# The order list of the attention and convolution stage, written anew

## The chip, the cores and the metric

The kernel runs on one core of one Trainium2 chip. The metric is the device time of one execution in microseconds (us). The profile shows five engines: TensorE (PE, with its weight loads as PEld), VectorE (DVE), ScalarE (ACT), GpSimd (POOL) and SyncE (SP), which here issues the transfers. Each engine works through its own instructions in order; semaphores connect them. Times inside the execution are counted from the start of the profiled span.

## The reference

One layer of a diffusion backbone is computed in float32 for 128 context tokens and 512 latent tokens of width 1024. In its middle stands a mixer that runs attention and a short convolution side by side on the same projection:

```python
q = _rms(q.reshape(b, s, N_HEADS, HEAD_DIM), q_norm)     # 8 heads of 64, 2 kv heads
k = _rms(k.reshape(b, s, N_KV, HEAD_DIM), k_norm)
...
attn = _block_attention(q_r, k_all, v_all)               # blocks of 128 queries, 640 keys for latents
y_conv = gb * _short_conv(gc * u, conv_w)                # width 3, 512 channels
merged = jnp.concatenate([_rms(attn, attn_out_norm), _rms(y_conv, conv_out_norm)], axis=-1)
return merged @ w_out, k, v
```

Around it, `_layer` computes the modulation `mod = silu(cond) @ w_ada + b_ada` (called ada below), two normalisations, and a SwiGLU feed-forward part with the weights `w_gate_up` and `w_down`. The context reads only context keys; latent queries attend to 128 cached context keys and 512 latent keys in one softmax.

## The kernel before

Every float32 product of large matrices is made of three matmuls of values split into a rounded high part and a remainder (`wh`/`wl` for weights, `hH`/`hL` for tokens; `split`, L150 to L152, writes the high part on ACT and the rest on DVE). The program has four stages: loading, ada and the query projection; then attention and convolution mixed; then the output projection; then the feed-forward part, which takes more than half of the time. The change lies in the second stage alone, which runs from about 60 to 256 us.

In that stage the order of TensorE's work is written out by hand in the string `SEQ` (L39 to L49). A loop at the end of the stage's code walks through it and calls one function for each entry:

```python
for x in SEQ.split():
    if "." in x:
        n, i = (int(y) for y in x[1:].split("."))
        {"S": att_s, "T": att_t, "O": att_o}[x[0]](units[n], i)
    else:
        steps[x[0]](int(x[1:]))
```

TensorE follows the list to the letter. What the steps ask of ACT, DVE, POOL and SP is put in order by a scheduler that goes by priorities, so a step moved in the list may also move work on those engines among other work. The entries are:

- `k0` to `k4`: keys and values of one block of 128 tokens (4 is the context): 24 matmuls (`kv_mm`), the norm of the heads, the split `osq` (L659 on ACT, L660 on DVE), and the store of the values. `c0` does the split alone for the cached keys (`ck`). `K` and `C` turn the split keys by transposes (L667) into `KA`/`KB`, evicted at L669 and L670.
- `q` splits the queries (no TensorE work), `Q` turns them (L703, evicted by ACT at L704).
- `a`, `t`, `o`: attention of the context (scores L917, exponential L928, transposes L936, products L947).
- `Su.h`: scores of unit u (16 units: four blocks, two kv heads, two pairs of heads each) for the head h of its pair (L835). DVE takes the max (L841), ACT scales it (L842) and takes the exponential (L845), DVE the reciprocal (L847), and the scaling is done on DVE for head 0 (L851), on ACT for head 1 (L849).
- `Tu.g`: transposes of the probabilities (L862) for key blocks 0 and 1, 2 and 3, or 4, and their split `ph`/`pl`.
- `Ou.g`: products with the values (L879). Behind `Ou.2` ACT evicts the unit (L886). Each second unit ends its pair of units: two transfers `es` on SP (L894, L895) exchange the halves of the partitions, DVE adds (L900, L901), ACT squares (L902).
- `r`: the row sums of the squares (L954) with the chain of the inverse root behind it, which starts with `ms` (L163).
- `F1`: the next filler from the convolution (L723 to L725; nine, nine and six matmuls for each half of the tokens) or a piece of ada (L394, L446, L785). Their order among themselves is fixed.

Few PSUM buffers are to be had: one score tile `ps` (so the next `S` waits until the exponential has read the one before), two tiles `pt` for all transposes, one `po`, three `pc`. Of `ph` and `pl` there are two each.

Of the kernel before, what the change touches and what calls it, by code (L numbers as in the profile page):

```python
# [37 lines left out]
XB = 3  # L38
SEQ = ('k1 c0 q4 k4 C0 k0 K4 Q4 q0 a0 F1 k2 a1 K0 t0 k3 t1 o0 K1 F1 Q0 o1 K2 F1 K3 F1 S0.0 F1 F1 S0.1 '  # L39
# [10 lines left out]
GCUT = [0, 6, 12, 17, 22]  # L50
GB = 3
SOP = [20, 0]
# [39 lines left out]
def build(ctx, tc, x_prompt, x_sample, c, cache_k, cache_v, c_ctx, norm_mix, norm_ffn, w_ada, b_ada,  # L92
# [875 lines left out]
    def rms_of(t):  # L968
        if t == CTX or t >= 0:
# [5 lines left out]
             "a": ctx_s, "t": ctx_t, "o": ctx_o, "r": att_rms}  # L975
    for x in SEQ.split():
        if "." in x:
# [404 lines left out]
```

## Time and profile before

| what | us |
| --- | --- |
| median of 3 runs | 751.99 (751.41 to 752.06) |
| the profiled execution | 752.85 |
| its span, first to last instruction | 751.1 |
| PE busy | 732.7 |
| PEld busy | 657.4 |
| DVE busy | 529.0 |
| ACT busy | 374.8 |
| POOL busy | 49.2 |

The granted clock of TensorE was 1.000. Busy times are sums over the whole span. In the rows of a timeline the columns are the start, the duration, the engine, the line, the operation with the tiles written and read, and in brackets the idle time before it and what ended that. A row of waits names who waited, for whom, the total, the number of times and the longest.

### The profile page before, as it was taken

The page shows a single profiled execution, that of the slowest core. Times are in us where ns is not written, and L with a number is a line of the kernel's source. Part 1 is how long each engine was busy: PE and PEld are TensorE (multiplying, and loading weights), DVE is VectorE, ACT ScalarE, POOL GpSimd, SP SyncE. Part 2 cuts the span into 40 slices and gives each one's busy share as a digit, 9 for nine tenths or more (in the row PEclk, how much of TensorE's full clock was granted, in tenths as well). Part 3 has the DMA queues.
Part 4 walks back from the last instruction along what each step waited for, and adds up shares of the span by engine and source line. Part 5 has one row for each costly group of instructions (what it writes and reads, how often), then busy time and mean ns, then how long its engine had stood idle before and what let it go on. Part 6 is the DMA issues. An engine that isn't in the chain of part 4 may idle for free.

```text
span 751.1 us, 11645 instructions
## 1 busy us (share of the span) xinstructions
PE 732.7 (98%) x4556; PEld 657.4 (88%) x4556; DVE 529.0 (70%) x905; ACT 374.8 (50%) x701; POOL 49.2 (7%) x85
## 2 busy tenths in 40 slices
PE   7899989999999999999999999999999999999997
PEld 5568878988988887899998799998889998899986
DVE  5557877676666798788868768765568766677653
ACT  5346878667666534775552135553125641255510
POOL 2402201011010120100000000000000000000000
PEclk9999999999999999999999999999999999999999
DMA  9995133522532464032325313233113132123312
GB/s 288 275 251 174 43 113 93 175 92 93 165 102 92 134 230 135 1 113 56 111 65 197 91 57 113 57 113 120 49 57 109 61 113 84 57 65 104 100 69 85
DMA packets 101387, 84.50 MB, mean 113 GB/s; under 512 B 3502, under 2 KB 81650, under 8 KB 101332
## 3 DMA queue, kind: packets, MB, share of 16 engines
q1 hardware_dynamic: 100980, 83.39, 36.1%
q0 software_dynamic: 352, 0.37, 0.4%
q8 instruction: 36, 0.59, 0.3%
q14 instruction: 19, 0.16, 0.1%
HBM read 79.68 MB, written 2.75 MB: 110 GB/s over the span
## 4 chain that ended last, share of the span: by engine, by line
PE 85%; DVE 4%; ACT 4%; DMA 4%; issue 1%; SPq 1%; POOL 0%; ACTq 0%
PE pf L155 19%; PE pf L156 19%; PE pf L157 19%; PE pc L723 3%; PE pc L725 3%; PE pc L724 3%; PE po L879 2%; PE pt L862 2%; PE ps L835 2%; PE pc L394 2%; PE ph L156 2%; PE ph L157 2%; PE ph L155 2%; DMA af<-in_w_ada_dram 1%; SPq L329 1%
## 5 line engine op out<-in xcount | busy, mean ns | idle before, releaser
L151 ACT ACTIVATE wh<-wf 128x1024 fp32r<-128x1024 f32 (+1 forms) x68 | 65.8, 970 | 109.4 <-PE pf L157 69.3
L152 DVE TENSOR_TENSOR wl<-wf,wh 128x1024 fp32r<-128x1024 f32 (+1 forms) x58 | 68.6, 1185 | 59.9 <-ACT wh L151 46.2
L155 PE MATMUL pf<-B,wh 128*128 128x320 f32 x288 | 89.1, 310 | 0.0
L157 PE MATMUL pf<-B,wl 128*128 128x320 f32 x288 | 89.1, 309 | 0.0
L156 PE MATMUL pf<-B,wh 128*128 128x320 f32 x288 | 89.0, 309 | 0.0
L155 PE MATMUL pf<-wh,gT 128*128 128x512 f32 (+1 forms) x225 | 86.9, 386 | 0.0
L155 PE MATMUL pf<-T,wh 128*128 128x320 f32 x280 | 86.8, 310 | 0.0
L156 PE MATMUL pf<-wl,gT 128*128 128x512 f32 (+1 forms) x225 | 86.5, 385 | 0.0
L156 PE MATMUL pf<-T,wh 128*128 128x320 f32 x280 | 86.5, 309 | 0.0
L157 PE MATMUL pf<-T,wl 128*128 128x320 f32 x280 | 86.5, 309 | 0.0
L157 PE MATMUL pf<-wh,gT 128*128 128x512 f32 (+1 forms) x225 | 86.5, 384 | 0.0
L151 ACT ACTIVATE wh<-sx 128x1024 fp32r<-128x1024 f32 x40 | 42.4, 1060 | 61.6 <-DVE sx L206 22.8
L152 DVE TENSOR_TENSOR wl<-sx,wh 128x1024 fp32r<-128x1024 f32 x40 | 49.0, 1224 | 28.2 <-ACT wh L151 24.7
L723 PE MATMUL pc<-hH,wh 128*128 128x320 f32 x192 | 61.1, 318 | 0.0
L725 PE MATMUL pc<-hH,wl 128*128 128x320 f32 x192 | 59.3, 309 | 0.0
L724 PE MATMUL pc<-hL,wh 128*128 128x320 f32 x192 | 59.3, 309 | 0.0
L157 PEld LDWEIGHTS pf<-B,wl 128*128 128x128 f32 x288 | 54.1, 188 | 0.1
L155 PEld LDWEIGHTS pf<-B,wh 128*128 128x128 f32 x288 | 54.1, 188 | 0.1
L156 PEld LDWEIGHTS pf<-B,wh 128*128 128x128 f32 x288 | 54.1, 188 | 0.1
L155 PEld LDWEIGHTS pf<-T,wh 128*128 128x128 f32 x280 | 52.5, 188 | 0.7 <-ACT u L1212 0.4
L156 PEld LDWEIGHTS pf<-T,wh 128*128 128x128 f32 x280 | 52.6, 188 | 0.0
L157 PEld LDWEIGHTS pf<-T,wl 128*128 128x128 f32 x280 | 52.6, 188 | 0.0
(302 smaller groups left out, 1670.0 us busy)
## 6 DMA issues: line engine op xcount, KB each, us to landing
wf<-in_w_gate_up_dram SPq DMA_DIRECT2D x44, 512.0 KB, 4.1
aw<-in_w_ada_dram SPq DMA_DIRECT2D x24, 512.0 KB, 4.0
wf<-in_w_down_dram SPq DMA_DIRECT2D x20, 512.0 KB, 3.8
wf<-in_w_in_dram SPq DMA_DIRECT2D x18, 512.0 KB, 5.5
af<-in_w_ada_dram SPq DMA_DIRECT2D x32, 256.0 KB, 6.3
x<-in_x_sample_dram SPq DMA_DIRECT2D x8, 512.0 KB, 6.1
wf<-in_w_out_dram SPq DMA_DIRECT2D x8, 512.0 KB, 4.3
wf<-in_w_ada_dram SPq DMA_DIRECT2D x8, 512.0 KB, 3.7
```

The source lines that it names most:

```text
L151: act.activation(hi, src, AF.Copy)
L152: dve.tensor_tensor(lo, src, f32(hi), ALU.subtract)
L155: pe.matmul(out, lh, rh, start=start, stop=False, skip_group_check=more)
L156: pe.matmul(out, lh, rl, start=False, stop=False, skip_group_check=more)
L157: pe.matmul(out, ll, rh, start=False, stop=stop, skip_group_check=more)
L394: pe.matmul(out[CG * g:CG * (g + 1)], cp[:, k], w, start=(k < 4), stop=(k >= KD - 4), skip_group_check=True)
L723: pe.matmul(acc, wh[:, k], hH[k][:, c0:c0 + n], start=(k == 0), stop=False)
L724: pe.matmul(acc, wh[:, k], hL[k][:, c0:c0 + n], start=False, stop=False)
L725: pe.matmul(acc, wl[:, k], hH[k][:, c0:c0 + n], start=False, stop=(k == KD - 1))
L835: pe.matmul(s2[:, g, :320], q, kk[:, v, P + g * 320:P + (g + 1) * 320], start=(i == 0), stop=(i == 1))
L862: pe.transpose(tp[:, i, h], u[3][h][:, kt * P:(kt + 1) * P], ident)
L879: pe.matmul(ov, w, x[:, i].rearrange("p a q -> p (a q)"), start=(g == 0 and i == 0 and n == 0), stop=(last and i == len(kts) - 1 and n == 1))
```

## The change

The string `SEQ` is replaced. It has the same 244 entries, 84 of them `F1`; some fifty stand one to four places earlier or later. No function, size or buffer is changed. Its beginning and one line of its end:

```diff
-SEQ = ('k1 c0 q4 k4 C0 k0 K4 Q4 q0 a0 F1 k2 a1 K0 t0 k3 t1 o0 K1 F1 Q0 o1 K2 F1 K3 F1 S0.0 F1 F1 S0.1 '
-       'q1 F1 F1 S1.0 F1 T0.0 S1.1 T0.1 T0.2 O0.0 F1 O0.1 O0.2 S2.0 T1.0 F1 T1.1 T1.2 S2.1 O1.0 F1 F1 '
...
-       'O12.2 S14.0 T13.0 T13.1 F1 S14.1 F1 F1 T13.2 F1 O13.0 F1 O13.1 S15.0 F1 F1 O13.2 S15.1 r2 T14.0 '
...
+SEQ = ('c0 k1 q4 k4 C0 k0 K4 Q4 a0 q0 F1 k2 K0 a1 t0 k3 t1 K1 o0 F1 Q0 o1 K2 K3 q1 F1 S0.0 F1 F1 F1 S0.1 F1 '
+       'F1 S1.0 T0.0 F1 S1.1 T0.1 T0.2 O0.0 F1 O0.1 O0.2 S2.0 T1.0 F1 T1.1 T1.2 S2.1 O1.0 F1 F1 r4 S3.0 Q1 '
...
+       'S13.0 O11.2 T12.0 T12.1 F1 O12.0 F1 S13.1 F1 T12.2 O12.1 F1 S14.0 T13.0 T13.1 F1 O12.2 F1 S14.1 F1 '
+       'O13.0 F1 O13.1 T13.2 S15.0 F1 r2 F1 T14.0 S15.1 O13.2 T14.1 F1 F1 F1 T14.2 F1 F1 F1 O14.0 O14.1 '
...
```

Three places show what becomes of it on the engines.

The first is the head of the latent attention. On TensorE, from K2 to S0.0 (`osq_1015` is the split of block 2, `osq_1097` of block 3; `ps_1201` and `ps_1208` are the score tiles of S0.0), the rows were

```order
L667 MATMUL pt_1170<-identr_210,osq_1015 128x128 x4
L723 MATMUL pc_963<-hH_57_199,wh_686 128x320
L724 MATMUL pc_963<-hL_65_207,wh_686 128x320
L725 MATMUL pc_963<-hH_57_199,wl_687 128x320
L723 MATMUL pc_963<-hH_58_200,wh_686 128x320
L724 MATMUL pc_963<-hL_66_208,wh_686 128x320
L725 MATMUL pc_963<-hH_58_200,wl_687 128x320
L667 MATMUL pt_1184<-identr_210,osq_1097 128x128 x4
```

and are now, again on TensorE from K2 on,

```order
L667 MATMUL pt_1170<-identr_210,osq_1015 128x128 x4
L667 MATMUL pt_1177<-identr_210,osq_1097 128x128 x4
L723 MATMUL pc_963<-hH_57_199,wh_686 128x320
L724 MATMUL pc_963<-hL_65_207,wh_686 128x320
L725 MATMUL pc_963<-hH_57_199,wl_687 128x320
L723 MATMUL pc_963<-hH_58_200,wh_686 128x320
L724 MATMUL pc_963<-hL_66_208,wh_686 128x320
L725 MATMUL pc_963<-hH_58_200,wl_687 128x320
L835 MATMUL ps_1208<-KA_729,qT_1142 128x320 x2
```

The six matmuls of the filler moved from between the two turns to behind them, and S0.0 follows at once.

On DVE at the same place, around the max of S0.0 (L841; `wl_1478` and `wl_1484` are the low parts of the same weights), the rows were

```order
L152 TENSOR_TENSOR m_176_737<-of_1119,m_175_736 128x256
L152 TENSOR_TENSOR wl_1478<-wf_1475,wh_1477 128x1024
L841 TENSOR_REDUCE nsr_1206<-ps_1201 128x1
L900 TENSOR_TENSOR of_1119<-t_267_1158,es_1160 64x256
L901 TENSOR_TENSOR of_1119<-t_267_1158,es_1160 64x256
L847 RECIPROCAL nsr_1206<-nsr_1206 128x1
L851 TENSOR_SCALAR pr_1209<-pr_1209,nsr_1206 128x640
```

and on DVE they are now

```order
L152 TENSOR_TENSOR m_176_737<-of_1126,m_175_736 128x256
L841 TENSOR_REDUCE nsr_1213<-ps_1208 128x1
L643 TENSOR_TENSOR pl_1194<-of_698,tab_589 128x16x16
L900 TENSOR_TENSOR of_1126<-t_267_1158,es_1160 64x256
L901 TENSOR_TENSOR of_1126<-t_267_1158,es_1160 64x256
L645 TENSOR_TENSOR pr_1192<-pr_1192,pl_1194 128x512
L847 RECIPROCAL nsr_1213<-nsr_1213 128x1
L152 TENSOR_TENSOR wl_1484<-wf_1481,wh_1483 128x1024
L851 TENSOR_SCALAR pr_1216<-pr_1216,nsr_1213 128x640
```

The weights' low part moved from ahead of the max to between the reciprocal and the scaling; two steps of the rotary positions (L643, L645) of `q1` came in between.

The second place is the end of unit 11. On SP, this piece of the difference shows the two transfers `es` of units 10 and 11 and the loads around them:

```order
-L228 DMA aw_2745<-in_w_ada_dram 128x2x512
-L228 DMA aw_2749<-in_w_ada_dram 128x2x512
-L894 DMA es_2768<-t_584_2631 64x2x128
-L895 DMA es_2768<-t_584_2631 64x2x128
+L228 DMA aw_2734<-in_w_ada_dram 128x2x512
+L228 DMA aw_2738<-in_w_ada_dram 128x2x512
 L228 DMA wf_3113<-in_w_out_dram 128x2x512
-L228 DMA aw_2927<-in_w_ada_dram 128x2x512
-L228 DMA aw_2931<-in_w_ada_dram 128x2x512
+L894 DMA es_2779<-t_593_2668 64x2x128
+L895 DMA es_2779<-t_593_2668 64x2x128
```

The load `wf_3113` of the output weights stood behind the two transfers and stands ahead of them now.

On DVE the rows from the max of S13.0 to that of S13.1 (`ps_2753` and `ps_2826` are their scores; L252 makes the low part of output weights) were

```order
L841 TENSOR_REDUCE nsr_2758<-ps_2753 128x1
L252 SCALAR_TENSOR_TENSOR wl_3090<-wf_3087,vec_187,wh_3089 128x512 x2
L847 RECIPROCAL nsr_2758<-nsr_2758 128x1
L851 TENSOR_SCALAR pr_2761<-pr_2761,nsr_2758 128x640
L152 TENSOR_TENSOR pl_2793<-pt_2787,ph_2792 128x512
L152 TENSOR_TENSOR pl_2802<-pt_2796,ph_2801 128x512
L900 TENSOR_TENSOR of_2523<-t_584_2631,es_2768 64x256
L152 TENSOR_TENSOR pl_2823<-pt_2819,ph_2822 128x256
L841 TENSOR_REDUCE nsr_2831<-ps_2826 128x1
```

and on DVE they are now, from the two L252 to the same max,

```order
L252 SCALAR_TENSOR_TENSOR wl_3090<-wf_3087,vec_187,wh_3089 128x512 x2
L841 TENSOR_REDUCE nsr_2769<-ps_2764 128x1
L152 TENSOR_TENSOR pl_2793<-pt_2787,ph_2792 128x512
L152 TENSOR_TENSOR pl_2802<-pt_2796,ph_2801 128x512
L847 RECIPROCAL nsr_2769<-nsr_2769 128x1
L851 TENSOR_SCALAR pr_2772<-pr_2772,nsr_2769 128x640
L900 TENSOR_TENSOR of_2523<-t_593_2668,es_2779 64x256
L841 TENSOR_REDUCE nsr_2831<-ps_2826 128x1
```

The two L252 moved ahead of S13.0's max, and the split `pl_2823` of T12.2, which stood between the addition (L900) and S13.1's max, is gone from there.

The third place is r2 (L954) on TensorE. Its rows from the products of O13.2 to the second tile of T14 (`pt_3044`) were

```order
L835 MATMUL ps_3017<-KA_729,qT_2492 128x320 x2
L835 MATMUL ps_3017<-KB_730,qT_2492 128x320 x2
L954 MATMUL pt_3029<-ones_174,osq_2524 128x1
L862 MATMUL pt_3035<-ident_77,pr_2871 128x128
L862 MATMUL pt_3035<-ident_77,pr_2910 128x128
L862 MATMUL pt_3035<-ident_77,pr_2871 128x128
L862 MATMUL pt_3035<-ident_77,pr_2910 128x128
L862 MATMUL pt_3044<-ident_77,pr_2871 128x128
```

and on TensorE they are now, from r2 to the first transpose of T14.0,

```order
L954 MATMUL pt_2996<-ones_174,osq_2524 128x1
L723 MATMUL pc_3002<-hH_51_193,wh_2730 128x320
L724 MATMUL pc_3002<-hL_59_201,wh_2730 128x320
L725 MATMUL pc_3002<-hH_51_193,wl_2731 128x320
L723 MATMUL pc_3002<-hH_52_194,wh_2730 128x320
L724 MATMUL pc_3002<-hL_60_202,wh_2730 128x320
L725 MATMUL pc_3002<-hH_52_194,wl_2731 128x320
L723 MATMUL pc_3002<-hH_53_195,wh_2730 128x320
L724 MATMUL pc_3002<-hL_61_203,wh_2730 128x320
L725 MATMUL pc_3002<-hH_53_195,wl_2731 128x320
L862 MATMUL pt_3012<-ident_77,pr_2876 128x128
```

A filler of nine matmuls now stands between r2 and T14.0, whose two tiles came right behind r2 before.

15 rows, old and new, of the table SEQ are left out of this document.

## The prediction

> **What bounds the kernel now.** I read the page first (its first rows and its chain), then a table of windows over the stage that the list orders, then TensorE's waits there.
>
> ```profile
> span 751.1 us, 11645 instructions
> PE 732.7 (98%) x4556; PEld 657.4 (88%) x4556; DVE 529.0 (70%) x905; ACT 374.8 (50%) x701; POOL 49.2 (7%) x85
> PE 85%; DVE 4%; ACT 4%; DMA 4%; issue 1%; SPq 1%; POOL 0%; ACTq 0%
> ```
>
> TensorE is busy for all but 18.4 us, and 85% of the chain that ended last is its own. A new order of the same work can only win from those 18.4 us, and only from the part that lies in this stage. The windows below give span, then busy time (and count) of PE, PEld, DVE, ACT and POOL, the granted clock, the DMA share and GB/s. The stage runs from about 60 to 256 us.
>
> ```profile
> 60.00:92.00 32.00, 29.23 (x229) 27.31 (x227) 25.80 (x81) 24.18 (x65) 9.43 (x12) 1.00 0.30 87
> 92.00:111.00 19.00, 16.86 (x113) 14.24 (x113) 15.46 (x28) 13.09 (x28) 1.52 (x2) 1.00 0.39 118
> 111.00:200.00 89.00, 88.88 (x641) 79.55 (x640) 59.76 (x121) 63.91 (x137) 10.54 (x19) 1.00 0.36 114
> 200.00:256.00 56.00, 54.95 (x393) 48.63 (x393) 37.30 (x77) 35.50 (x77) 3.58 (x9) 1.00 0.38 123
> 256.00:291.00 35.00, 34.40 (x158) 27.85 (x156) 33.63 (x56) 18.02 (x35) 7.21 (x6) 1.00 0.58 194
> ```
>
> PE's idle time is 2.77 + 2.14 + 0.12 + 1.05 = 6.1 us in the stage, most of it before 111 us. Behind the stage DVE is 96% busy for 35 us. What PE waits for in the stage (total, times, longest):
>
> ```profile
> PE ps L835 <- ACT pr L845: 2.4, 4, 1.0
> PE pt L703 <- ACT qT L704: 1.0, 1, 1.0
> PE pt L936 <- ACT wh L151: 0.7, 1, 0.7
> PE pt L862 <- DVE ms L163: 0.4, 1, 0.4
> PE ps L917 <- ACT pr L928: 0.3, 1, 0.3
> PE pt L667 <- ACT osq L659: 0.3, 1, 0.3
> PE pt L667 <- DVE osq L660: 0.2, 1, 0.2
> ```
>
> The largest is the score step S (L835) that waits for the exponential of the score before (L845), since there is one score tile. Matmul ends are modelled, so short stalls show only as gaps of the weight loads. These rows of PEld are for 92 to 111, 111 to 160, 160 to 200, and the last two for 200 to 256 us:
>
> ```profile
> PEld ps L835 <- ACT pr L845: 2.9, 4, 1.2
> ...
> PEld ps L835 <- ACT pr L845: 0.5, 2, 0.4
> ...
> PEld ps L835 <- ACT pr L845: 0.2, 1, 0.2
> ...
> PEld ps L835 <- ACT pr L845: 0.9, 2, 0.7
> ...
> PEld pt L862 <- DVE ms L163: 0.6, 1, 0.6
> ```
>
> **The change, part by part.** Nothing is added or removed: 244 entries each, and the same 84 fillers. A filler is 9 or 6 matmuls of the convolution, or a piece of ada. What is moved changes what I call cover: PE's work between a step and the step that needs its result. The price of a place is latency minus cover.
>
> *The head, to T0.0.* The rows that carry it:
>
> ```profile
> 66.44 0.40 ACT L659 ACTIVATE osq<-ck 128x256 fp32r<-128x256 f32 x1
> 69.97 0.43 DVE L660 TENSOR_TENSOR osq<-pr,osq 128x256 fp32r<-128x256 f32 x1 [0.28 <-ACT osq L659]
> 89.23 0.43 DVE L660 TENSOR_TENSOR osq<-pr,osq 128x256 fp32r<-128x256 f32 x1
> 89.78 0.46 PE L667 MATMUL pt<-identr,osq 128*128 128x128 f32 x4
> 92.15 1.22 DVE L152 TENSOR_TENSOR wl<-wf,wh 128x1024 fp32r<-128x1024 f32 x1
> 93.28 0.82 DVE L841 TENSOR_REDUCE nsr<-ps 128x1 f32<-128x640 f32 x1
> 94.11 0.31 PE L724 MATMUL pc<-hL,wh 128*128 128x320 f32 x1
> 94.25 0.31 PE L725 MATMUL pc<-hH,wl 128*128 128x320 f32 x1
> 94.52 0.88 ACT L845 ACTIVATE pr<-ps,nsr,rq 128x640 f32<-128x640 f32 x1
> 95.55 0.56 PE L835 MATMUL ps<-KA,qT 128*128 128x320 f32 x2 [0.99 <-ACT pr L845]
> 95.95 0.45 PE L835 MATMUL ps<-KB,qT 128*128 128x320 f32 x2
> 99.73 0.83 ACT L849 ACTIVATE pr<-pr,nsr 128x640 f32<-128x640 f32 x1 [0.50 <-DVE nsr L847]
> ```
>
> Step c0 (the cached keys' split) comes first, so `osq<-ck` moves ahead of the stage on ACT and DVE; C0 no longer waits (0.3 + 0.2 us). K4, behind k0, then arrives that much earlier and its own osq (done at 70.40) is soon the limit: I take 0.5 us of the gain through to Q4 and bound it by 0.2 and 0.8. K0 goes ahead of a1 and fills its 0.3 us wait, but that takes 0.3 us of cover from t1, whose wait of 0.7 us stays: 0 to 0.3, I take 0.3. So t1 starts 0.8 us earlier.
>
> K3 now stands right behind K2 with no filler between. K3's osq ended at 89.66 while its matmuls began at 89.78, and the six matmuls taken out are 6 x 0.147 = 0.9 us (0.147 is the distance of matmul starts where they run behind one another: nine take 1.3). Of the 0.9 the slack of 0.1 goes off: 0.8 if the osq moves with PE. Its ACT half stands behind the evictions of Q0, so it will move less: I take a stall of 1.0, bounds 0.3 and 1.2. That gives back the gain: +0.2.
>
> Then S0.0. Before, its max (L841) stood behind a 1.22 us split (L152 `wl`) on DVE; the split is now behind the reciprocal, so the max starts up to 0.9 us sooner, and three fillers stand between S0.0 and S0.1 instead of two (cover 2.2 to 3.5 us). S0.1 began at 95.55 after 0.99 us of idling: this stall goes, and with the weight load's share (the longest of PEld's four) it is 1.2, which brings the head to −1.0. The split now delays S0.0's normalisation by 1.2 us, which nobody needs before T0.0. T0.0 itself moves ahead of a filler, right behind S1.0; the L849 that it needs ended at 100.56, 4.2 us behind S0.1's matmuls (95.95 + 0.45), and its cover falls from 4.7 to 3.3: a new stall of 0.8 to 1.0. It fills the time in which S1.1 used to wait for S1.0's exponential (of PEld's 2.9 us I give it 0.9). Of PEld's 2.9 us in four waits, 2.9 − 1.2 − 0.9 = 0.8 is left, at S1.0 and S2.0; with the earlier max it shrinks by some 0.6. Head: −0.5 −0.3 +1.0 −1.2 +0.0 −0.6 = **−1.6** (bounds −2.8 and 0).
>
> *Middle and r2.* Between S6.0 and S6.1 one filler more (2.3 to 3.6 us of cover): the 0.4 us wait goes. S10.0 moves behind two fillers and T9's transposes (2.4 to 5.8): 0.2 goes. r2, the row sums before T14.0, moves one filler (1.3 us) ahead, so the 0.6 us wait of T14.1's tile for `ms` (L163) goes; I take 0.5. Covers that shrink stay over the exponential's latency, which was 2.1 us from the max's start (93.28) to L845's end (95.40) at S0.0 and up to 0.9 more where the max waits, 2.1 to 3.0: S7.1 to S8.0 falls from 5.7 to 3.5, S11.1 to S12.0 from 5.1 to 3.1, S14.1 to S15.0 from 6.0 to 3.7. Cost nothing there; if that cover is gone, see the first rival. Term: −0.4 −0.2 −0.5 = **−1.1** (−1.5 and −0.3).
>
> *S12 to S14.* SP now issues a 512 KB load ahead of the two `es` transfers of units 10 and 11, ACT both halves of L251 ahead of the eviction (L886) that they need, and DVE L900 directly ahead of S13.1's max.
>
> ```profile
> DMA to landing us min/median/max: 2.0/2.4/4.5
> 215.19 0.88 SPq L228 DMA_DIRECT2D aw<-in_w_ada_dram  x2
> 216.70 0.60 SPq L894 DMA_DIRECT2D es<-t  x1
> 218.15 0.44 SPq L228 DMA_DIRECT2D wf<-in_w_out_dram  x1
> 216.57 0.71 ACT L251 ACTIVATE wh<-wf,vec 128x512 fp32r<-128x512 f32 x1
> 221.22 0.42 DVE L900 TENSOR_TENSOR of<-t,es 64x256 f32<-64x256 f32 x1 [0.76 <-DMA es<-t]
> 221.90 0.81 DVE L841 TENSOR_REDUCE nsr<-ps 128x1 f32<-128x640 f32 x1
> 228.10 0.56 PE L835 MATMUL ps<-KA,qT 128*128 128x320 f32 x2 [0.46 <-ACT pr L845]
> ```
>
> Behind two loads this `es` took 4.5 us (216.70 to 221.2) against a median of 2.4, so about 1.05 per load. Now 0.7 (L251) + 0.4 (the load's issue) + 1.05 (a third load) = 2.2 us later, or 1.1 if queues do not add. L900's end moves from 221.64 to 222.7 or 223.8, and L841 with it, less the 0.4 us split that stood between them. S14.0 needs S13.1's exponential; its cover grows by 0.3. So S14.0 stalls 0.4 to 1.5 us, I take 0.8. Against it S14.1's wait goes (0.7 by its weight load), having one filler more, and T13.0 keeps its wait. Term: +0.8 −0.7, about **0** (−1.1 and +1.2). In the Trainium skill, "DMA: Bandwidth & Descriptors", section "Queues, rings and completion order", descriptors of one issuing engine are consumed in ring order on each DMA engine; by that the full 2.2 us counts and the sum would be 0.7 us worse. The trace agrees as far as the 4.5 us landing behind two loads goes.
>
> *Behind the stage* order and work stay nearly the same: 0. DVE's near-full stretch (33.63 of 35.00 us) starts with work that waits for the last O and the last convolution, so it starts earlier with the stage's end; 0.6 us of PE idling there bounds it, −0.3 to +0.6.
>
> Sum: −1.6 −1.1 +0 +0 = −2.7. The profiled execution took 752.85 us (span 751.1 and 1.75 around it), 0.86 above the median of 751.99; 752.85 − 2.7 = 750.15 there, and 749.3 as a median.
>
> **The rivals.** *Covers too short* (slower). The list shortens some ten distances, T7.0's from 6.3 to 4.1, T0.0's from 4.7 to 3.3, the score steps above, and at O8.0, O9.0 and O12.0 the time for the eviction between two units from 2.4 to 3.9 down to 2.0 to 2.2. T0.0's needed latency of 4.2 shows that such distances can bind. If ACT and DVE serve them 0.5 us later than now at nine places, 4.5 us come back: −2.7 + 4.5 = +1.8, **753.8**. It decides (no gain) from 0.3 us a place. For it: ACT and DVE are 76% and 81% busy from 60 to 92 us. Against it: from 111 to 200 us they are 72% and 67% busy, and PE idles 0.12 us in 89.
>
> *The gain is absorbed* (same). DVE at 96% from 256 to 291 us could be the bound whenever the stage ends; then all that is won before turns into waiting there, **752.0**. For it: the DVE row. Against it: PE is 98% busy in the same 35 us, so DVE is not ahead of it by being the only limit.
>
> *Only the head works.* The S12 to S14 term comes out at its bad end, +1.2, and r2's wait moves on to the next reader of that tile (+0.5): −2.7 + 1.2 + 0.5 = −1.0, **751.0**, hardly measurable.
>
> **How the numbers follow.** A measurement of this kernel can tell about 0.2%, 1.5 us. Forecast (749.3, its own range 747.4 to 750.5) 0.58; covers too short 0.22; absorbed 0.10; only the head 0.10. The head at its good end and the rest as summed give 752.0 − 1.2 − 2.7 = 748.1, with the middle and S12 to S14 good too 746.6; I put the low end at 747.2. The high end takes in about half of the first rival, up to +1.5: 753.5. Faster: 0.58 and a fifth of the last case, 0.60; slower: the first rival and a little of the others, 0.24; same 0.16.
>
> **What would show it.** Right: no wait at C0 or S0.1, a wait of about 1 us at K3 (L667) and at T0.0 (L862 for L849), L835's total for L845 down from 2.4 to about 1.5, none at L862 for L163; `es` of units 10 and 11 landing 1 to 2 us later and S14.0 waiting. Wrong: waits of L835, L862 or L879 between 111 and 200 us, where there were none; a stage shorter by over 2 us while the span stays (absorbed); PE waits for `wl` (L252) behind 256 us.

## The result, and the profile after

The changed kernel took 747.49 us (median of 4 runs, 747.37 to 747.79) against 751.99 us (751.41 to 752.06): the ratio is 0.9942, with a 95% interval of 0.9925 to 0.996. It is 4.5 us faster. The forecast was 2.7 us faster, 749.3; the time lies in the stated range (747.2 to 753.5), near its low end. One later run of the kernel before took 2537.83 us and stands in no ratio below.

The page of the profiled execution after, the same rows as before:

```profile
span 745.8 us, 11640 instructions
PE 729.5 (98%) x4556; PEld 657.5 (88%) x4556; DVE 529.8 (71%) x905; ACT 375.6 (50%) x701; POOL 48.6 (7%) x85
PE 85%; DVE 6%; DMA 3%; ACT 3%; issue 2%; POOL 1%; SPq 0%; ACTq 0%; DVEq 0%; POOLq 0%
```

Work and bound are the same; only PE's idle time is less. The windows after, with the columns as in the prediction:

```profile
60.00:92.00 32.00, 29.26 (x227) 27.27 (x226) 26.89 (x83) 23.58 (x64) 9.45 (x12) 1.00 0.28 76
92.00:111.00 19.00, 17.34 (x121) 15.17 (x120) 14.51 (x26) 13.74 (x31) 2.07 (x2) 1.00 0.35 111
111.00:200.00 89.00, 89.00 (x647) 79.87 (x646) 62.13 (x125) 65.16 (x138) 10.05 (x19) 1.00 0.38 117
200.00:256.00 56.00, 55.05 (x389) 49.91 (x388) 38.23 (x76) 38.07 (x81) 5.92 (x11) 1.00 0.41 132
```

Idle time in the second and fourth windows fell little (2.14 to 1.66 us, 1.05 to 0.95), in the first hardly at all. The windows are fixed in time while the work in them moved, so they do not show the gain well. What shows it is where the stage begins and ends. Its first matmul, and the first one behind its last step, stand here, first of before, then of after:

```profile
60.69 0.28 PE L155 MATMUL pc<-wh,hH 128*128 128x256 f32 x1
255.66 0.39 PE L155 MATMUL ph<-wh,m 128*128 128x512 f32 x1
```

```profile
59.26 0.28 PE L155 MATMUL pc<-wh,hH 128*128 128x256 f32 x1
251.01 0.39 PE L155 MATMUL ph<-wh,m 128*128 128x512 f32 x1
```

Before, the stage took 255.66 − 60.69 = 194.97 us; after, 251.01 − 59.26 = 191.75. That is 3.2 of the 5.3 us by which the two spans differ, and 0.6 more lie behind the stage. The other 1.4 us lie ahead of it, where neither list has a say, and the profiles name 1.1 of them: waits for the ada pieces of the loading stage. First before, then after, for 20 to 60 us:

```profile
PE pc L394 <- DMA af<-in_w_ada_dram: 1.9, 3, 1.2
```

```profile
PE pc L394 <- DMA af<-in_w_ada_dram: 0.8, 1, 0.8
```

That is one execution against another: in the twelve runs below the stage begins at 59.2 to 59.8 us, with the old beginning of the list as with the new. The profiled execution of before was a late one, 0.86 us over its median. So I compare stages by their length, and whole kernels by medians.

What PE waits for in the stage after (total, times, longest):

```profile
PE pt L936 <- ACT wh L151: 0.9, 1, 0.9
PE pc L723 <- DVE modt L448: 0.9, 1, 0.9
PE ps L835 <- ACT pr L845: 0.9, 1, 0.9
PE pt L862 <- ACT pr L849: 0.7, 1, 0.7
PE pt L703 <- ACT qT L704: 0.7, 1, 0.7
PE ps L835 <- DVE KB L670: 0.3, 1, 0.3
PE pt L667 <- ACT osq L659: 0.3, 1, 0.3
PE pt L703 <- DVE pl L152: 0.2, 1, 0.2
```

The score step's waits for the exponential fell from four (2.4 us) to one (0.9). T14.1's wait for `ms` (L163) and C0's are gone; the 0.3 us for `osq` are K3's now (forecast). Three more are new: L862 for L849 (T0.0, forecast), L835 for `KB` (S0.0, not forecast), and L723 for `modt` (a filler behind T14.2, not forecast).

### The profile page after: what moved, and what is told of

Read it like the earlier page. It is cut to its first block, busy times and chain, and to the rows that moved or that the text cites. A ratio compares the mean times of both kernels' runs of the same rounds, so it can differ in the third digit from the quotient of the medians.

```text
span 745.8 us, 11640 instructions
## 1 busy us (share of the span) xinstructions
PE 729.5 (98%) x4556; PEld 657.5 (88%) x4556; DVE 529.8 (71%) x905; ACT 375.6 (50%) x701; POOL 48.6 (7%) x85
## 4 chain that ended last, share of the span: by engine, by line
PE 85%; DVE 6%; DMA 3%; ACT 3%; issue 2%; POOL 1%; SPq 0%; ACTq 0%; DVEq 0%; POOLq 0%
PE pf L155 19%; PE pf L156 19%; PE pf L157 19%; PE pc L723 3%; PE pc L725 3%; PE pc L724 3%; PE pt L862 3%; PE po L879 2%; PE ps L835 2%; PE pc L394 2%; PE ph L156 1%; PE ph L157 1%; PE ph L155 1%; DMA es<-t 1%; DMA af<-in_w_ada_dram 1%
## 5 line engine op out<-in xcount | busy, mean ns | idle before, releaser
L152 DVE TENSOR_TENSOR wl<-wf,wh 128x1024 fp32r<-128x1024 f32 (+1 forms) x58 | 69.2, 1195 | 59.2 <-ACT wh L151 45.2
L723 PE MATMUL pc<-hH,wh 128*128 128x320 f32 x192 | 61.0, 318 | 0.9 <-DVE modt L448 0.9
L156 PEld LDWEIGHTS pf<-T,wh 128*128 128x128 f32 x280 | 52.6, 188 | 0.0
```

The costliest lines, as they stand in the source:

```text
L152: dve.tensor_tensor(lo, src, f32(hi), ALU.subtract)
L156: pe.matmul(out, lh, rl, start=False, stop=False, skip_group_check=more)
L723: pe.matmul(acc, wh[:, k], hH[k][:, c0:c0 + n], start=(k == 0), stop=False)
```

## Experiments

The parts of the new list were put into the kernel before, one at a time, cut where both lists have handled the same steps. Behind S14.1 the count of fillers has to come out even: before, two stand there, in p_late and p_cov none, in p_end three, and in the changed kernel one. Beside the medians (each against the kernel before on the same chip; the ratios are worked out from all runs, not from the medians) stands the length of the stage in the profiled execution, 194.97 before and 191.75 after.

| kernel | what it has | median, us | against before, us | ratio (95%) | stage, us |
| --- | --- | --- | --- | --- | --- |
| p_swap | entries 1 and 2 new | 751.36 | −0.57 | 0.9991 (0.9982 to 1.0000) | 194.65 |
| p_head | entries 3 to 52 new | 752.23 | +0.30 | 1.0003 (0.9994 to 1.0012) | 195.10 |
| p_headswap | entries 1 to 52 new | 751.04 | −0.96 | 0.9991 (0.9981 to 1.0000) | 194.82 |
| p_mid | to O8.1 new | 751.13 | −0.80 | 0.9989 (0.9979 to 0.9998) | 194.38 |
| p_late | S10.0 to S14.1 new | 750.07 | −1.86 | 0.9976 (0.9966 to 0.9986) | 193.18 |
| p_es | S10.0 to O11.2 new | 751.03 | −0.97 | 0.9988 (0.9978 to 0.9997) | 194.26 |
| p_cov | T12.0 to S14.1 new | 750.73 | −1.27 | 0.9982 (0.9973 to 0.9992) | 193.78 |
| p_end | behind S14.1 new | 751.36 | −0.92 | 0.9992 (0.9983 to 1.0001) | 194.96 |
| after_again | all new | 747.93 | −4.49 | 0.9940 (0.9926 to 0.9953) | 191.66 |
| a_o13 | all new, O13.2 earlier | 747.15 | −4.85 | 0.9940 (0.9922 to 0.9959) | 190.93 |
| a_k3b | all new, a filler back at K3 | 747.18 | −5.10 | 0.9936 (0.9920 to 0.9953) | 190.68 |
| a_best | both | 746.88 | −5.54 | 0.9928 (0.9916 to 0.9941) | 190.54 |

The four parts p_headswap, p_mid, p_late and p_end make up the whole list, and their medians add to −0.96 −0.80 −1.86 −0.92 = −4.54 us, against −4.5 for the whole. That this fits so closely is chance: each interval reaches about 0.7 us to either side, and by the four ratios the sum is −3.9. The two profiles of the result, cut at the same three places, divide the stage's 3.2 us like this: the head 0.8 shorter (52.58 to 51.77), the middle 0.9 (70.92 to 70.02), S10 to S14 2.0 (46.56 to 44.54), and the end 0.5 longer (24.91 to 25.43). So the largest piece lies in S10 to S14, where the forecast had 0.2, and in the whole list the end of the stage gains nothing.

The head's own length repeats: 52.6 to 52.9 us in the six profiles with the old head, 51.6 to 51.8 in the four with the new one.

### The head

```diff
-SEQ = ('k1 c0 q4 k4 C0 k0 K4 Q4 ...
+SEQ = ('c0 k1 q4 k4 C0 k0 K4 Q4 ...
```

> The kernel before with its first two entries alone exchanged (c0 ahead of k1). Theory A (the 1.4 us by which the stage starts earlier in the profile of the changed kernel are a matter of when the ada pieces of the loading stage land, and not of the list): C0 loses its 0.5 us of waiting, K4 and Q4 keep or take over most of it, the stage (from k1's first matmul to the end of O15.2, 194.6 us before) gets 0.2 to 0.6 us shorter, and its start lies anywhere between 59.2 and 60.8 us. Rival B (the exchange itself brings the start forward, by what ACT does ahead of the stage): the start is at 59.3 us here and in every kernel that has the exchange, and at 60.7 in every kernel without.

The start was 59.41 us here, and 59.20, 59.50, 59.76 in p_mid, p_late and p_head, which have the old beginning: the exchange does not bring the start forward, and rival B falls. Summed step by step (each distance between the starts of two matmuls, less what it is where nothing holds them up; I call this the steps' sum), the stage is 0.67 us ahead behind Q4; at S1.1 only 0.16 of that is left. At the stage's end it was 0.32.

```diff
-... Q4 q0 a0 F1 k2 a1 K0 t0 k3 t1 o0 K1 F1 Q0 o1 K2 F1 K3 F1 S0.0 F1 F1 S0.1 q1 F1 F1 S1.0 F1 T0.0 S1.1 ...
+... Q4 a0 q0 F1 k2 K0 a1 t0 k3 t1 K1 o0 F1 Q0 o1 K2 K3 q1 F1 S0.0 F1 F1 F1 S0.1 F1 F1 S1.0 T0.0 F1 S1.1 ...
```

> The kernel before with the new order only from its third entry to the thirteenth filler (head without the exchange: a0, K0, K1, K2 K3 together, three fillers behind S0.0, T0.0 behind S1.0). By the prediction's terms: 1.1 us shorter (0.5 of the 1.6 belongs to c0). By the account of the two traces (waits summed up step by step): 0.1 to 0.4 us shorter only, with K2, K3 and S0.0 waiting 1.2 to 1.5 us together instead of the 1.0 assumed.

No gain at all. Alone, this part is worth nothing; K2, K3 and S0.0 lose 1.9 us where the list of before lost 0.6.

> The kernel before with the new order from the first entry to the thirteenth filler, the exchange of c0 and k1 included. By the prediction: 1.6 us shorter. By the account of the two traces: 0.8 us shorter (stage 194.2), that is more than the exchange alone (0.32) and the rest of the head alone (0.13 longer) together, because what the head's K3 and S0.0 wait for (the evictions KB of L670 and the split osq of block 3) is also what C0's wait pushes back.

Together the two are worth 0.9 us at the thirteenth filler by the steps' sum (9.40 us of waiting before, 8.50 here), though neither alone has it: up to there the stage took 52.58 us before, 52.43 in p_swap, 52.69 in p_head, and 51.68 here. The runs' times can't tell this; the ratio is 0.9991 here and in p_swap, with nearly the same interval. The profiled execution ran at a granted clock of 0.949, so its stage length as a whole (194.82) is not compared with the others. The expectation of 0.8 held for the head; the 1.6 of the prediction did not.

Why the head gave less than forecast is seen in the profile after, from K3 to T0.0 (rows of PE, DVE and ACT in order of time):

```profile
87.00 0.85 PE L667 MATMUL pt<-identr,osq 128*128 128x128 f32 x4 [0.26 <-ACT osq L659]
87.84 0.42 DVE L900 TENSOR_TENSOR of<-t,es 64x256 f32<-64x256 f32 x1 [0.41 <-DMA es<-t]
88.74 0.76 DVE L670 CAST KB<-pt 128x256 fp32r<-128x256 f32 x2
89.56 0.41 PE L835 MATMUL ps<-KB,qT 128*128 128x320 f32 x1 [0.31 <-DVE KB L670]
90.21 0.82 DVE L841 TENSOR_REDUCE nsr<-ps 128x1 f32<-128x640 f32 x1
92.85 1.78 DVE L152 TENSOR_TENSOR wl<-wf,wh 128x1024 fp32r<-128x1024 f32 x1
95.23 0.81 DVE L841 TENSOR_REDUCE nsr<-ps 128x1 f32<-128x640 f32 x1
96.40 0.89 ACT L845 ACTIVATE pr<-ps,nsr,rq 128x640 f32<-128x640 f32 x1
97.43 0.56 PE L835 MATMUL ps<-KA,qT 128*128 128x320 f32 x2 [0.85 <-ACT pr L845]
99.10 0.55 PE L862 MATMUL pt<-ident,pr 128*128 128x128 f32 x3 [0.71 <-ACT pr L849]
```

K3 waits as forecast (for `osq`, 0.9 us by the steps' sum). Both `KB` evictions, 88.74, stand on DVE behind L900, which waits for its `es` transfer, and S0.0's second half waits for them: a step that the forecast did not name. S0.0's max is early now (90.21, no split ahead of it). But the split has only changed its victim. It runs from 92.85, takes 1.78 us here instead of 1.22, the scaling of S0.0 stands behind it, and S0.1's max comes at 95.23, 1.2 us behind the end of S0.1's matmuls at 94.07. So S1.0 waits 0.85 where S0.1 waited 0.99 before.

```diff
-... K2 K3 q1 F1 S0.0 F1 F1 F1 S0.1 ...
+... K2 F1 K3 q1 F1 S0.0 F1 F1 S0.1 ...
```

> The changed kernel with a filler put back between K2 and K3, taken from the three between S0.0 and S0.1. By the prediction (stall of 1.0 at K3 for want of cover; S0.1's third filler and the split moved behind S0.0's max worth 1.2): K3 no longer waits, S0.1 waits 0.2 to 0.4, the stage is 0.3 to 0.8 us shorter than the changed kernel's. Theory by the trace after: K2, K3 and S0.0 wait 1.4 us together there by the weight loads, and S1.0 another 1.1, because the 1.2 us split now stands ahead of S0.1's max instead of S0.0's; here the first falls to 0.3, S1.0's wait stays or goes as the split stands, and the stage is 0.5 to 1.5 us shorter. Rival: the wait moves on to S0.1 and S1.0 in full, as all of them wait for one chain on DVE, and the stage stays within 0.3 us.

The waits of PE in this kernel from 60 to 111 us:

```profile
PE pt L862 <- ACT pr L849: 1.2, 1, 1.2
PE pt L936 <- ACT wh L151: 0.9, 1, 0.9
PE ps L835 <- ACT pr L845: 0.9, 2, 0.6
PE pt L703 <- ACT qT L704: 0.7, 1, 0.7
PE pt L703 <- DVE pl L152: 0.2, 1, 0.2
```

The waits for `osq` and `KB` are gone. Behind them the waits at L835 stay at 0.9 in all and T0.0's grows from 0.7 to 1.2. The head is 0.64 us shorter, the stage 1.08 (the rest at T14.2, below). So the missing cover at K3 did cost about what it was forecast to cost, and the rival (all of it moves on) holds for half.

### The middle

```diff
-... S3.0 Q1 F1 F1 O1.1 O1.2 r4 T2.0 ... T5.1 S6.1 F1 O5.0 ... S7.1 F1 F1 F1 r0 O6.1 F1 O6.2 S8.0 ...
+... r4 S3.0 Q1 F1 T2.0 F1 O1.1 T2.1 ... T5.1 F1 O5.0 S6.1 ... S7.1 F1 F1 F1 S8.0 T7.0 T7.1 O6.2 ...
```

> The kernel before with the new order only from behind the thirteenth filler to O8.1. By the prediction: 0.4 us shorter (S6.1's wait). By the account of the two traces: 0.7 to 0.9 us shorter, the rest in many weight load gaps of 0.08 that fall away. Rival (covers too short): longer, with waits of L862 or L835 between 111 and 185 us.

The stage got 0.59 us shorter, the median 0.80. S6.1's 0.36 is the largest piece. The rest is several gaps of about 0.08 between steps. No wait of PE is left in the list of waits from 111 to 200 us: the rival of covers too short has no case here.

### S10 to S14

```diff
-... O11.1 F1 F1 S13.0 O11.2 F1 T12.0 T12.1 F1 O12.0 T12.2 S13.1 O12.1 F1 F1 O12.2 S14.0 T13.0 T13.1 F1 S14.1 F1 F1 T13.2 ...
+... F1 O11.1 S13.0 O11.2 T12.0 T12.1 F1 O12.0 F1 S13.1 F1 T12.2 O12.1 F1 S14.0 T13.0 T13.1 F1 O12.2 F1 S14.1 T13.2 ...
```

> The kernel before with the new order only from S10.0 to S14.1. By the prediction (S10.0's 0.2, and about 0 for S12 to S14): 0.2 us shorter, S14.0 waiting 0.4 to 1.5. By the account of the two traces: 1.7 to 2.0 us shorter, S14.0, S14.1, T13.0 and O12.0 without waits, the es transfers of units 10 and 11 landing about 3.3 us behind their issue since the two loads ahead of them were issued 3.6 us before and have drained.

1.79 us shorter, where the forecast had 0.2. In the profile after, SP's issues there, and on DVE the addition and the max that wait in a row:

```profile
210.97 0.88 SPq L228 DMA_DIRECT2D aw<-in_w_ada_dram  x2
214.15 0.37 SPq L228 DMA_DIRECT2D wf<-in_w_out_dram  x1
214.62 0.60 SPq L894 DMA_DIRECT2D es<-t  x1
217.91 0.42 DVE L900 TENSOR_TENSOR of<-t,es 64x256 f32<-64x256 f32 x1 [0.43 <-DMA es<-t]
218.25 0.81 DVE L841 TENSOR_REDUCE nsr<-ps 128x1 f32<-128x640 f32 x1
```

The order is the one foretold: the load ahead of `es`, and L900 ahead of the max. But `es` took 214.62 to 217.91, 3.3 us, not 4.5 and one more load. The two ada loads went out 3.65 us ahead of it, not 1.5. The DMA packets in the traces show what that does. When `es` was issued, 960 KB of the loads ahead of it were still to be moved before, and 790 KB after, although one more load stood ahead. The first packet of `es` began 2.5 us behind the issue before and 2.2 after, when most of those loads had been moved. And before, the load `wf` issued behind `es` ran among its packets, which took 1.3 us, against 0.7 after. S13.1, with its matmuls ended at 218.07, lost only 0.18 at the max. Two halves of the part were then run alone:

```diff
-... S10.0 F1 F1 T9.0 ... O11.1 F1 F1 S13.0 O11.2   (then as before)
+... F1 F1 T9.0 T9.1 S10.0 ... F1 O11.1 S13.0 O11.2
```

> The kernel before with the new order from S10.0 to O11.2 alone: the eviction of units 10 and 11 and their es transfers stand as in the changed kernel (the 512 KB load of output weights ahead of them), the covers behind T12.0 as before. Theory A (what the stretch S12 to S14 gains is the es transfers' shorter way: fillers moved ahead of O11.2 let the two ada loads drain first): es lands about 3.3 us behind its issue instead of 4.5, L900 waits less, and most of the 1.8 us of the late part are there (stage 1.2 to 1.6 us shorter than before). Rival B (the longer covers behind T12.0 are what counts): 0.2 to 0.5 us shorter. By the prediction (a third load adds 1.05 us): es lands 5.5 us behind its issue and the stage gets 0.3 to 1.0 us longer.

```diff
-... O11.2 F1 T12.0 T12.1 F1 O12.0 T12.2 S13.1 O12.1 F1 F1 O12.2 S14.0 T13.0 T13.1 F1 S14.1 F1 F1 T13.2 ...
+... O11.2 F1 T12.0 T12.1 F1 O12.0 F1 S13.1 F1 T12.2 O12.1 F1 S14.0 T13.0 T13.1 F1 O12.2 F1 S14.1 T13.2 ...
```

> The kernel before with the new order from T12.0 to S14.1 alone: the covers of the changed kernel, the es transfers as before, right behind the two ada loads and ahead of the output weights' load. Theory A (es): the landing stays at 4.5 us, S13.1's max stays behind L900, and S14.0 waits; the stage is 0.2 to 0.6 us shorter than before. Rival B (covers): S14.1's and T13.0's waits are gone and the stage is 1.2 to 1.8 us shorter.

In p_es the stage is 0.71 us shorter, in p_cov 1.19; together that is the 1.79 of p_late within 0.1. Neither theory has it alone, and the shorter way of `es` is not what pays in p_es. On DVE there:

```profile
220.00 0.81 DVE L841 TENSOR_REDUCE nsr<-ps 128x1 f32<-128x640 f32 x1
220.74 0.41 DVE L900 TENSOR_TENSOR of<-t,es 64x256 f32<-64x256 f32 x1
```

S13.1's max stands ahead of L900 there, so whenever `es` lands, the max does not wait for it. S14.1 still waits 0.5 us in this kernel. In p_cov `es` is issued at 215.83 behind two loads issued at 214.32:

```profile
215.83 0.60 SPq L894 DMA_DIRECT2D es<-t  x1
220.12 0.42 DVE L900 TENSOR_TENSOR of<-t,es 64x256 f32<-64x256 f32 x1 [0.54 <-DMA es<-t]
221.16 0.82 DVE L841 TENSOR_REDUCE nsr<-ps 128x1 f32<-128x640 f32 x1 [0.17 <-PE ps L835]
```

4.3 us, nearly as before, and yet nothing is lost: a filler stands ahead of S13.1, and its max waits for the scores, not for L900. The wait of S14.1, which has a filler more, is gone too. So S13.1's max no longer waits for `es` in p_es, in p_cov and in the whole list: by its place in DVE's queue, by later scores, or by both later scores and an earlier landing. That is a small part of the gain, though. By the steps' sum S14.0, the next step behind that max, waited 0.28 us before and 0.01 after. The larger parts are other waits, and each goes with one of the two halves. Among the gaps of the weight loads from 208 to 256 us, these three stand in the kernel before:

```profile
PEld ps L835 <- ACT pr L845: 0.9, 2, 0.7
PEld pt L862 <- ACT pr L849: 0.4, 1, 0.4
PEld po L879 <- DVE pl L152: 0.3, 1, 0.3
```

In the whole list none of them is left. In p_es these are:

```profile
PEld ps L835 <- ACT pr L845: 0.9, 2, 0.7
PEld pt L862 <- ACT pr L849: 0.4, 1, 0.4
```

and in p_cov this one:

```profile
PEld po L879 <- DVE pl L152: 0.3, 1, 0.3
```

They are S14.1's wait for the exponential (0.6 us of gain by the steps' sum), T13.0's for the scaling of S13 (0.3) and O12.0's for the split of T12 (0.4). The covers of p_cov take the first two, the order of p_es the third, and with it 0.2 each at S10.0 and S12.1.

The loads ahead of `es` do cost time. With no load in the 3.5 us before it, `es` landed in 2.1 us (issued at 238.25 in the kernel before). With the load `wf` directly ahead it took 3.2 to 3.5 us in seven kernels, and in the order of before 4.2 to 4.6 us in seven. But whole loads are the wrong thing to count: the order with three loads ahead was the faster one. What differs between the two is how much of the loads was still to be moved at the issue (770 to 820 KB against 950 to 990 KB), and whether `wf` came behind `es`.

### The end of the stage

```diff
-... S14.1 F1 F1 T13.2 F1 O13.0 F1 O13.1 S15.0 F1 F1 O13.2 S15.1 r2 T14.0 T14.1 F1 F1 F1 T14.2 F1 F1 O14.0 ... F1 F1 O15.0 O15.1 F1 O15.2')
+... S14.1 F1 F1 F1 O13.0 F1 O13.1 T13.2 S15.0 F1 r2 F1 T14.0 S15.1 O13.2 T14.1 F1 F1 F1 T14.2 F1 F1 F1 O14.0 ... F1 O15.0 F1 O15.1 O15.2')
```

> The kernel before with the new order only behind S14.1 (r2 a filler earlier, T14.0 ahead of S15.1, O13.2 behind it, one filler more behind T14.2, the last O steps). By the prediction: T14.1's wait of 0.5 goes and nothing else changes, 0.5 us shorter. By the account of the two traces: T14.1's wait goes, but a filler behind T14.2 waits about 1.2 us for L448, so the stage gets 0.4 to 0.8 us longer; the part behind the stage gets 0.5 to 0.7 us shorter (494.8 instead of 495.4 us), because the output weights' splits (L252) stand a little earlier, so that in sum the time stays within 0.3 us.

T14.1's wait is gone: from S14.1's filler to T14.1 the steps lost 0.93 us before and 0.34 here. The stage as a whole is no shorter in this execution (194.96), since 0.3 us went at S0.0, where the list is the old one; behind S14.1 it took 24.44 us against 24.91. The median is 0.92 lower, with an interval that includes no gain. Part of that lies behind the stage, 495.02 us against 495.42, where PE waited once for `wl` (L252) instead of twice. This part is not settled: the part behind the stage took 494.79 in the first profile of the changed kernel and 495.53 in the second. Over all profiles it took 495.0 on average in the six with the new end of the list, and 495.4 in the seven with the old one at a full clock.

The expected wait behind T14.2 did not come in p_end, but it does in the whole list. After, in order of time:

```profile
237.62 0.42 DVE L900 TENSOR_TENSOR of<-t,es 64x256 f32<-64x256 f32 x1 [0.98 <-DMA es<-t]
239.00 0.18 DVE L448 TENSOR_REDUCE modt<-pc 128x8 f32<-128x32 f32 x1
239.23 0.39 PE L723 MATMUL pc<-hH,wh 128*128 128x320 f32 x1 [0.95 <-DVE modt L448]
```

The ada sums (L448) stand behind L900 on DVE, L900 waits for `es`, and the filler needs the accumulator that L448 reads. Why `es` lands late here and not in p_end is shown in the last section.

```diff
-... S15.0 F1 r2 F1 T14.0 S15.1 O13.2 T14.1 ...
+... S15.0 F1 r2 F1 O13.2 T14.0 S15.1 T14.1 ...
```

> The changed kernel with one step more moved: O13.2 stands ahead of T14.0 and S15.1 instead of behind them. In the changed kernel a filler behind T14.2 waits 0.9 us (1.25 by the weight loads) for the sums of an ada piece (L448), which stand on DVE behind L900 and L901, and these wait for the es transfers that O13.2 starts. Theory: O13.2 comes 1.2 us earlier, so do es, L900 and L448, the wait falls to 0 to 0.3, and the stage is 0.8 to 1.2 us shorter than the changed kernel's. Rival: that filler waits for something else (ACT's eviction, the ada load), and nothing is gained.

```profile
235.90 0.41 DVE L900 TENSOR_TENSOR of<-t,es 64x256 f32<-64x256 f32 x1
237.24 0.42 DVE L901 TENSOR_TENSOR of<-t,es 64x256 f32<-64x256 f32 x1 [0.93 <-DMA es<-t]
238.22 0.18 DVE L448 TENSOR_REDUCE modt<-pc 128x8 f32<-128x32 f32 x1
```

L448 comes 0.8 us earlier, no wait of PE between 200 and 256 us is left in that execution's list of waits, and the stage is 0.83 us shorter. The chain is the right one. L901 still waits for the second half of `es`, and by the steps' sum 0.4 of the 1.2 to 1.3 us is left.

### Both edits, and the changed kernel again

> The changed kernel with both small edits: the filler back between K2 and K3, and O13.2 ahead of T14.0. Theory (two waits far apart that do not meet): the stage shortens by 0.6 in the head and by about 0.8 at T14.2, 190.1 to 190.4 us against 191.8, and the median lies 1.0 to 1.5 us under that of the changed kernel run beside it. Rival (the wait behind T14.2 shrinks with the filler put back already, or what is won in the stage is lost behind it): within 0.3 us of the filler alone (stage 190.7).

> The changed kernel once more, beside the last one and the kernel before on the same chip: 747.3 to 747.8 us. Its profile tells what repeats from execution to execution: by the theory the stage takes 191.6 to 191.9 us again and the part behind it 494.7 to 494.9, while its start lies anywhere between 59.2 and 60.7.

On one chip, a_best took 746.88 us and the changed kernel 747.93: 1.05 us less, the fastest of all, though its interval (0.9916 to 0.9941) overlaps that of the changed kernel. The head kept its gain (7.65 us of waiting at the thirteenth filler, against 8.41), but the wait behind T14.2 was back with 0.7 us, so the stage is only 0.14 shorter than with the filler alone: of the two theories, the rival is the nearer. The stage of the changed kernel repeated within 0.1 us (191.66).

## Why the prediction was right, point by point

**The direction, the bound and the place** were right: PE's idle time in the stage was to be won, work stayed, and the gain went through to the end. The rival that DVE absorbs it behind the stage falls (that part took no longer with the new list than with the old), and so does the one of covers too short: no new wait arose at S8.0, S12.0, S15.0, O8.0, O9.0 or O12.0.

**The head** was forecast at −1.6 and gave −0.9. C0 to Q4 came as computed (−0.5; 0.67), t1 too (−0.8 in all; 0.83), and K2 to S0.0 cost +1.2 instead of +1.0, with `KB` in it that was not named. The term that was mis-sized is S0.0 to S2.0: −1.8 was forecast (1.2 and 0.6), −1.1 came. The 1.2 at S0.1 came in full, but S1.0 waits more than before, not less. The sentence that failed is that the moved split delays something "which nobody needs before T0.0". It delays the scaling of S0.0 and, in the same queue, S0.1's max.

**The middle and r2** were forecast at −1.1. p_mid gave −0.6 by its stage and −0.8 by its median, S6.1's 0.4 and small gaps; r2's 0.6 came with 0.59. New and unforeseen is the wait behind T14.2, 1.2 to 1.3 us in the whole list.

**S12 to S14** was the wrong term: about 0 was forecast (−1.1 to +1.2), −1.8 came for S10 to S14, 0.2 of it at S10.0. One half of the term was right: S14.1's wait went (0.6 against the 0.7 forecast). The step that failed is the other half, +0.8: that `es` lands 1.1 to 2.2 us later, S13.1's max with it, and S14.0 waits. `es` landed 1.2 us sooner, and S14.0's wait went from 0.28 to 0.01. The price of 1.05 us for each load came from one row (4.5 us behind two loads), and a third load was counted on top, without asking how much of the others would be left by then: the same move that put the load ahead moved the ada loads from 1.5 to 3.65 us ahead. And the term let S13.1's max wait behind L900, where the step S13.1 itself had moved behind a filler. Three waits were left out of it: T13.0's, which was said to stay (0.3), O12.0's (0.4) and S12.1's (0.2). On the ring order of one issuing engine, in the Trainium skill's "DMA: Bandwidth & Descriptors" ("Queues, rings and completion order"): the packets fit it, since the first one of `es` began when 1494 of the 1536 KB ahead had begun in the changed kernel, and 886 of 1024 before. But the 0.7 us that I drew from it did not show.

**The sum**: −0.9 −0.7 −1.8 −0.6 +1.2 is −2.8 in the stage by these single parts, −3.2 by the profiles of the whole; with the 0.4 us behind the stage it comes to about −3.6. The medians say −4.5. Some 0.2 us of the rest is the head of the profiled execution of before, the shortest of the six with the old head. For the remaining 0.7 us no row of a profile was found; starts of the stage that differ by some 0.6 us between executions are as large.

That the time fell into the range is in part luck. The head's and S12 to S14's terms were off in opposite directions (0.7 too much, 1.8 too little), S12 to S14 lies outside its own bounds, and the 1.2 us behind T14.2 were not in the sum at all.

## What to carry to other kernels

When an instruction moves in an in-order queue, do not stop at the one that it no longer delays: walk down to the next instruction that someone waits for, since the split that left S0.0's max stood ahead of S0.1's. A transfer's latency behind loads is not a count of loads but depends on how much of them is still to be moved; take it from rows with the same distance, or leave it wide. And where a list is cut into parts, run two neighbours together as well: by the profiles the exchange and the rest of the head gave 0.3 and nothing alone, and 0.9 together up to the same place. Last, medians of parts that add up to that of the whole prove little when each is known to 0.7 us; the profiles, cut at the same places, said that one of the four gains nothing in the whole.

## What the runs showed of the hardware

The last `es` transfers of the stage (two of 64 KB) landed in 2.1 us in p_end with a load 5.1 us ahead of them, and in 3.3 us in the changed kernel, and 3.4 when it was run again, with no load issued in the 6.3 us before. So loads are not the cause here. The DMA packets in the traces show another one: a 16 KB transfer of instructions (queue q8 of the profile) runs once near this place in each of the fourteen profiles, for 0.9 to 1.4 us.

| kernel | `es` issued at | instructions moved from, to | first half landed behind its issue, us |
| --- | --- | --- | --- |
| p_end | 238.93 | 238.88, 239.81 | 2.1 |
| after | 234.29 | 235.17, 236.43 | 3.3 |
| after_again | 234.09 | 234.94, 236.30 | 3.4 |
| a_k3b | 233.69 | 234.41, 235.35 | 2.8 |
| a_o13 | 233.30 | 235.12, 236.00 | 2.1 |
| a_best | 232.54 | 234.95, 235.88 | 2.1 |

In a_o13 and a_best it is the second half that is late: issued 0.65 us behind the first, it made DVE wait until 3.3 and 3.8 us behind its own issue. In a_best 120 of the 128 packets of the second half had begun by 234.87; the other 8 began at 235.87 and later, as the transfer of instructions ended. In the changed kernel 15 of the 16 parts of the first half were complete at 236.00, and the last one only after 236.43. So a sixteenth of `es` waited until the instructions had been moved, and DVE waits for all of it. In p_end the instructions were through before the first packet of `es` (240.19); in the other eight profiles they came with its last packets or later, and the first half landed in 2.1 us. This is what set the wait behind T14.2: it is in the whole list and not in p_end, it is smaller in a_k3b, and it is nearly gone in a_o13 and 0.7 us in a_best, though both have O13.2 in the same place. No run moves that transfer on purpose; the fourteen profiles show only where it fell.
